# Two inverse matrices, the Fourier branch behind the first two at twice the pace, norm loads on ACT's queue, and an earlier recurrence

## The chip, the cores and the metric

One NeuronCore of a Trainium2 chip runs the whole layer. The metric is device time in microseconds (us) of one launch, lower is better. TensorE is the matmul engine (PE, its weight loads PEld), VectorE is DVE, ScalarE is ACT, GpSimd is POOL; SyncE (SP) starts most DMAs. Each engine works through its own instructions in order.

## What is computed

One layer of a hybrid encoder, 2048 positions, width 1024, all in float32. The normalised input goes through one projection, whose columns feed three branches:

```python
za, za_gate, z_rwkv, zb_gate, zq, zkv, zkr, zc_gate, z_merge = split_cols(h @ w_in, IN_SPLITS)
ya = fourier_mix(za, fourier_w) * silu(za_gate)         # 2-D DFT, real part, group map
zs = centred_shift(z_rwkv, mu_prev, mu_next)
yb = rwkv7_bidir(zs, ...) * silu(zb_gate)               # delta rule in both directions, then group norm
yc = mla(zq, zkv, zkr, ...) * silu(zc_gate)             # attention, 6 heads
g = sigmoid(z_merge)                                    # one gate per branch
merged = g0 * (ya @ proj_a) + g1 * (yb @ proj_b) + g2 * (yc @ proj_c)
out = rms_norm(x + merged @ w_out) * final_g
```

The scan of `rwkv7_bidir` is, per head and direction, `S = S * w + (S a) b^T + v k^T; y = S r`.

## The kernel before

Matmuls keep float32 precision by splitting operands in a high and a low part and adding three products (`mm3`), or run in float32 directly. A scheduler orders most instructions of each engine by priority over a simulated timeline; `after(n)` lowers (or raises) the priority of what it holds. Inside `manual_schedule` TensorE's order is the order of the program text, so a matmul that isn't ready holds all that follow.

**First part, input projection.** `inproj` loads 128 columns of the weights, splits them on ACT and GpSimd, and `project` makes one tile of 128 columns x 512 positions with 24 matmuls. The last 32 column groups (128 projections) run in `columns`, and other work is interleaved with them by hand: `pace` is called twice in each projection, and with `rate` 1 every second call, with `rate` 2 every call, makes one `step`, which advances the generator at the head of a list to its next `yield`. The generators are, in order, `units`, `recurrence`, and later `rwkv_out` and `phase3_early`.

**units** prepares the scan in chunks of 64 positions. 24 windows (three pairs of heads, eight windows of 256 positions) are worked in both directions: low-rank matmuls from a tile `ul`, decay and keys on ACT, VectorE and GpSimd (`unit_decay`; `kds` sums the keys of both directions for the bonus), gram matrices (`unit_gram`), all written to `X_d` in DRAM. Then come the triangular **inverses**, one for each pair of heads: a matrix M of 128 lanes x 64 x 64 is loaded from `X_d`, 62 pairs of VectorE instructions (`tmp`, `M`) solve it in place, and it is written back from GpSimd's queue. One tile M serves all three. They have low priority (`late`), and three of their steps are made for every step of **fourier**, which runs at rate 1 in the same stretch: two halves of 128 columns, each with folds on VectorE, matmuls with DFT matrices loaded as `dm`, and a gate multiplication.

**Second part, attention.** `phase2` works 96 units of 128 queries: scores for 2048 keys (`sc`, evicted and maximised by VectorE as `S`), exp on ACT, 16 transposes `tp` evicted as `PT` (two of four groups by VectorE, `ptd`, two by ACT), value matmuls `av` in pieces. Two steps are made in each unit. `units` waits twelve of them (`wait2`), then **recurrence** goes through 32 chunks in three steps each (`seq_r`, `seq_u`, `seq_s`, `seq_y`), with X and W loaded a chunk ahead, and sets `merged`. Then **rwkv_out** adds the two directions `y_d`, normalises each head's 64 channels with matmuls for the sums (`mu`, `var`), adds the bonus, multiplies the gate, in eight blocks of 256 positions, six steps each, loads started from SP.

**Third part.** Branch projections, merge gates, output projection, final norm. The change doesn't touch it.

Of the kernel before, what the change touches and what calls it, by code (L numbers as in the profile page):

```python
# [9 lines left out]
F32 = mybir.dt.float32  # L10
# [3 lines left out]
ALU = mybir.AluOpType  # L14
# [76 lines left out]
class Trunk:  # L91
    def __init__(self, tc, ins, out, stop=99):
# [266 lines left out]
    def columns(self):  # L359
# [180 lines left out]
    def units(self):  # L540
        tc, nc = self.tc, self.nc
        with tc.tile_pool(name="un", bufs=1, side="right", reuse_waits="tile") as up, \
# [10 lines left out]
            ul = self.unit_lora(opened[0], 0, up)  # L553
# [4 lines left out]
            for s in range(2 * len(wins) + 2):  # L558
# [5 lines left out]
                if s < 2 * len(wins):  # L564
# [5 lines left out]
                    wps = self.unit_lowrank(w, d, ul, gps)  # L570
                    item = self.unit_decay(w, d, wps, up, ge)
# [3 lines left out]
                if s < 2 * len(wins):  # L575
# [4 lines left out]
                    if s + 1 < 2 * len(wins):  # L580
                        ul = self.unit_lora(opened[n + d], 1 - d, up)
# [4 lines left out]
        with tc.tile_pool(name="inv", bufs=1, side="right", reuse_waits="tile") as ip:  # L586
            self.invs = [self.inverses(ip)]
            self.rate = 1
            for _ in self.fourier():
                for _ in range(3):  # L590
                    self.inv_step()
                yield
            while self.invs:
                self.inv_step()
        while not self.rest:
            yield
        for _ in range(self.wait2):
            yield

    def inv_step(self):  # L600
        if self.invs:
            try:
                next(self.invs[0])
            except StopIteration:
                self.invs.pop(0)
# [32 lines left out]
    def unit_lora(self, w, d, up):  # L638
        lo = up.tile([P, 2, UN], F32R, tag="ul", name=f'ul{w["p"]}{w["u"]}{d}', bufs=self.ulb)
        self.nc.sync.dma_start(lo.bitcast(F32), self.lo_d[:, d, :, w["sl"]].rearrange("n p t -> p n t"))  # L640
        return lo
# [9 lines left out]
    def unit_decay(self, w, d, wps, up, ge):  # L651
# [84 lines left out]
    def inverses(self, ip):  # L736
        nc, tc = self.nc, self.tc
        M = ip.tile([P, C, C], F32, name="M")
        tmp = ip.tile([P, 1024], F32, name="tmp")
        diag = M.rearrange("p s t -> p (s t)")[:, ::C + 1]  # L740

        def lanes(p, k):
            d, h, c = k // 4, k // 2 % 2, k % 2 * 16
            return (M[16 * k:16 * k + 16],
                    self.X_d[d][c:c + 16, :, p, 4 * C:5 * C].rearrange("c (h s) t -> c h s t", h=2)[:, h])

        for k in range(8):
            m, x = lanes(0, k)
            nc.sync.dma_start(m, x)
            yield  # L750
        for p in range(NP):
            with self.after(self.late):
                nc.gpsimd.memset(diag, 1.0)
            for j in range(1, C - 1):
                n = C - 1 - j
                with self.after(self.late):
                    tv = tmp[:, 0:j * n].rearrange("p (c i) -> p c i", i=n)
                    nc.vector.tensor_tensor(tv, M[:, 0:j, j:j + 1].to_broadcast([P, j, n]),  # L758
                                            M[:, j:j + 1, j + 1:C].to_broadcast([P, j, n]), ALU.mult)
                    nc.vector.tensor_tensor(M[:, 0:j, j + 1:C], M[:, 0:j, j + 1:C], tv, ALU.add)  # L760
                if j % 3 == 0:
                    yield
            with self.after(self.late):
# [733 lines left out]
```

## Time and profile before

| what | value |
|---|---|
| time, median of 3 runs (lowest to highest) | 2627.77 us (2625.58 to 2630.97) |
| time of the profiled execution | 2634.32 us, of which the span of the instructions is 2632.5 us |
| TensorE busy | 2504.7 us, 95% of the span |
| VectorE, ACT, GpSimd busy | 1737.4, 991.9, 848.0 us |
| TensorE clock granted, mean | 0.982 of full speed |
| DMA | 404.86 MB, mean 154 GB/s |

Busy time of TensorE is that of pipelined matmuls, so a busy engine need not be at its peak. Columns is the stretch from about 480 to 1402 us, attention from 1402 to 2263, the third part from there to the end.

### The profile page before, as it was taken

What the parts mean: (1) busy time and instruction counts of PE and PEld (TensorE: products, weight loads), DVE (VectorE), ACT (ScalarE), POOL (GpSimd) and SP (SyncE); (2) the same over time, 40 slices, a digit from 0 to 9 for tenths busy, and PEclk for the clock granted to TensorE, in tenths of its full rate; (3) what the DMA queues carried; (4) which work ended last, traced back from release to release, by engine and by line L of the source; (5) the groups of instructions that cost most, each with busy time, mean ns of one, the idle gap of its engine ahead of it and who ended that gap; (6) DMA issues with size and microseconds to landing.
All of it is one profiled execution on the core that took longest, in us unless ns stands there. A gap on an engine that the chain in (4) does not pass through costs nothing.

```text
span 2632.5 us, 46308 instructions
## 1 busy us (share of the span) xinstructions
PE 2504.7 (95%) x17295; PEld 2040.8 (78%) x17295; DVE 1737.4 (66%) x3432; ACT 991.9 (38%) x1929; POOL 848.0 (32%) x1124
## 2 busy tenths in 40 slices
PE   7989999999999999989998899999998899999998
PEld 6778887877777777768776688878876677799997
DVE  6236564388888859579398567766767787544444
ACT  6354443355555521111113333333355565322221
POOL 2244433355555511212220233323322220334342
PEclk9999999999999999999998899999999999999999
DMA  4353434477777774552733655665544311645452
GB/s 167 95 146 121 149 125 157 141 262 256 245 262 247 246 156 128 130 145 86 136 84 111 157 169 186 192 186 166 174 149 125 101 53 59 194 128 154 131 154 78
DMA packets 318443, 404.86 MB, mean 154 GB/s; under 512 B 56078, under 2 KB 225097, under 8 KB 317130
## 3 DMA queue, kind: packets, MB, share of 16 engines
q1 hardware_dynamic: 310762, 382.99, 49.0%
q0 software_dynamic: 7456, 18.91, 3.0%
q8 instruction: 137, 2.24, 0.4%
q14 instruction: 88, 0.72, 0.1%
HBM read 236.91 MB, written 164.89 MB: 153 GB/s over the span
## 4 chain that ended last, share of the span: by engine, by line
PE 38%; DVE 13%; DMA 8%; issue 4%; POOL 1%; ACT 1%; SPq 1%; DVEq 0%; POOLq 0%; ACTq 0%
PE av L1334 5%; PE tp L1322 4%; DVE M L760 4%; DVE tmp L758 4%; PE sc L142 3%; PE sc L144 2%; PE sc L143 2%; PE po L144 2%; PE po L143 2%; PE po L142 2%; PE p L144 2%; PE p L143 2%; PE p L142 2%; DVE S L1307 1%; PE mm L142 1%
## 5 line engine op out<-in xcount | busy, mean ns | idle before, releaser
L142 PE MATMUL mm<-hh,wh 128*128 128x512 f32 x1536 | 613.8, 400 | 6.5 <-ACT z L483 3.2
L144 PE MATMUL mm<-hh,wl 128*128 128x512 f32 x1536 | 604.0, 394 | 2.8 <-POOL wl L419 2.6
L143 PE MATMUL mm<-hl,wh 128*128 128x512 f32 x1536 | 605.2, 394 | 0.0
L142 PEld LDWEIGHTS mm<-hh,wh 128*128 128x128 f32 x1536 | 291.7, 190 | 72.1 <-ACT z L483 5.2
L144 PEld LDWEIGHTS mm<-hh,wl 128*128 128x128 f32 x1536 | 291.6, 190 | 65.1 <-POOL wl L419 4.1
L143 PEld LDWEIGHTS mm<-hl,wh 128*128 128x128 f32 x1536 | 291.9, 190 | 58.2 <-issue 1.0
L1307 DVE TENSOR_SCALAR_CACHE_REDUCE S<-sc 128x512 f32<-128x512 f32 x384 | 260.7, 688 | 73.2 <-PE sc L144 67.5
L419 POOL TENSOR_TENSOR wl<-wr,wh 128x256 fp32r<-128x256 f32 x192 | 172.2, 910 | 419.1 <-ACT wh L418 406.2
L1322 PEld LDWEIGHTS tp<-c_id,S 128*128 128x128 f32 x1536 | 192.9, 143 | 84.9 <-ACT PT L1033 14.5
L1322 PE MATMUL tp<-c_id,S 128*128 128x128 f32 x1536 | 237.8, 278 | 21.0 <-ACT S L1314 8.6
L1314 ACT ACTIVATE S<-S,m 128x2048 f32<-128x2048 f32 x96 | 192.2, 2003 | 161.7 <-DVE m L1312 161.7
L758 DVE TENSOR_TENSOR tmp<-M 128x62 f32<-128x62 f32 (+30 forms) x186 | 171.7, 923 | 96.5 <-DMA zm_d<-z 41.3
L142 PE MATMUL sc<-K,Q 96*128 96x512 f32 x384 | 188.4, 491 | 19.7 <-DVE S L1307 13.8
L1033 ACT ACTIVATE PT<-tp 128x512 f32<-128x512 f32 x192 | 113.2, 591 | 225.8 <-PE tp L1322 222.7
L1334 PE MATMUL av<-PT,V 128*64 128x256 f32 x1536 | 180.0, 385 | 0.0
L760 DVE TENSOR_TENSOR M<-M,tmp 128x62 f32<-128x62 f32 (+30 forms) x186 | 170.7, 918 | 5.8
L418 ACT ACTIVATE wh<-wr 128x256 fp32r<-128x256 f32 x192 | 74.4, 412 | 238.7 <-DMA wr<-in_w_in_dram 149.2
L144 PE MATMUL sc<-K,Q 96*128 96x512 f32 x384 | 155.4, 405 | 0.0
L143 PE MATMUL sc<-K,Q 96*128 96x512 f32 x384 | 154.8, 403 | 0.0
L483 ACT ACTIVATE z<-mm 128x512 f32<-128x512 f32 (+1 forms) x120 | 70.3, 589 | 217.7 <-PE mm L144 107.2
L1334 PEld LDWEIGHTS av<-PT,V 128*64 128x64 f32 x1536 | 105.4, 137 | 57.8 <-issue 11.2
L1432 POOL TENSOR_TENSOR g<-g 128x256 f32<-128x256 f32 x128 | 98.8, 774 | 143.2 <-DVE g L1430 100.6
(388 smaller groups left out, 4945.4 us busy)
## 6 DMA issues: line engine op xcount, KB each, us to landing
X_d<-X SPq DMA_DIRECT2D x96, 512.0 KB
sX<-X_d SPq DMA_DIRECT2D x64, 768.0 KB
wr<-in_w_in_dram SPq DMA_DIRECT2D x193, 128.0 KB
zm_d<-z SPq DMA_DIRECT2D x96, 256.0 KB
g<-zm_d SPq DMA_DIRECT2D x64, 384.0 KB
uu<-u_d SPq DMA_DIRECT2D x24, 512.0 KB
ul<-lo_d SPq DMA_DIRECT2D x48, 256.0 KB
sW<-V_d SPq DMA_DIRECT2D x128, 96.0 KB
```

What stands on the lines that cost most here:

```text
L142: mm(out, lh, rh, start=start, stop=False)
L143: mm(out, lh, rl, start=False, stop=False)
L144: mm(out, ll, rh, start=False, stop=stop)
L419: nc.gpsimd.tensor_tensor(wl[:, ks, :], wr, wh[:, ks, :].bitcast(F32), ALU.subtract)
L758: nc.vector.tensor_tensor(tv, M[:, 0:j, j:j + 1].to_broadcast([P, j, n]), M[:, j:j + 1, j + 1:C].to_broadcast([P, j, n]), ALU.mult)
L760: nc.vector.tensor_tensor(M[:, 0:j, j + 1:C], M[:, 0:j, j + 1:C], tv, ALU.add)
L1033: return self.nc.scalar.activation(out, src, AF.Copy)
L1307: nc.vector.tensor_scalar(u["S"][:, ks], sc, 1.0, -3.4e38, ALU.mult, ALU.max, accum_out=u["m4"][:, kb:kb + 1])
L1314: nc.scalar.activation(S, S, AF.Exp, scale=SM_SCALE, bias=m4[:, 5:6], accum_out=u["win"]["rs"][:, col:col + 1])
L1322: nc.tensor.transpose(tp[:, k, :], u["S"][:, (4 * g + k) * P:(4 * g + k + 1) * P], self.ident)
L1334: nc.tensor.matmul(av[64 * h:64 * h + 64, 0:QB], self.V[:, k, (2 * hp + h) * 64:(2 * hp + h + 1) * 64], PT[k // 4][:, k % 4, h, :], start= ...
L1432: nc.gpsimd.tensor_tensor(g, g, acc, ALU.add)
```

## The change

The three inverses get two tiles, M0 and M1 (`Ms`). Both are fetched at once when the units are done; the first two inverses run alone, one step at each step of the projections; the third pair's data is fetched into M0 during the second. After a gap of five steps the Fourier branch starts, at rate 2, with some steps added, and one step of the third inverse beside each of its own. `recurrence` starts its loads before it waits, and waits two steps instead of twelve. Loads of X come behind those of W. `ul` is loaded right behind the matmuls that free its buffer. One addition of the keys goes from GpSimd to VectorE. In the norm the loads go to ACT's queue, the addition of the two directions goes to GpSimd, a block ahead, and a step is added in each block. Once the recurrence is done, one of four PT groups is VectorE's instead of two. The scaling of the row sums `rs` moves behind the third piece of the value matmuls. The last gates are written from ACT's queue and projected in another order.

```diff
-        self.wait2 = 12
+        self.wait2 = 2
+        self.gap = 5
...
-        gates = [(O_ZCG + n * P, self.to_gate(self.gc_d[n], self.nc.gpsimd)) for n in range(3)]
+        gates = [(O_ZCG + n * P, self.to_gate(self.gc_d[n], self.nc.scalar)) for n in range(3)]
...
-        for tb in range(NTB):
+        for tbs in ((0, 1), (2, 3)):
             for w, consume in cols:
-                self.project(w, P, tb, consume, True)
+                for tb in tbs:
+                    self.project(w, P, tb, consume, True)
...
                     wps = self.unit_lowrank(w, d, ul, gps)
+                    if s + 1 < 2 * len(wins):
+                        ul = self.unit_lora(wins[n + d], 1 - d, up)
                     item = self.unit_decay(w, d, wps, up, ge)
...
-                    if s + 1 < 2 * len(wins):
-                        ul = self.unit_lora(opened[n + d], 1 - d, up)
...
-            self.invs = [self.inverses(ip)]
             self.rate = 1
+            Ms = [ip.tile([P, C, C], F32, name="M0")]
+            tmp = ip.tile([P, 1024], F32, name="tmp")
+            self.inv_fetch(Ms, 0, nc.sync)
+            yield
+            with tc.tile_pool(name="inv1", bufs=1, side="right", reuse_waits="tile") as ip1:
+                Ms.append(ip1.tile([P, C, C], F32, name="M1"))
+                self.inv_fetch(Ms, 1, nc.sync)
+                yield
+                yield from self.inverse(Ms, tmp, 0)
+                for n, _ in enumerate(self.inverse(Ms, tmp, 1)):
+                    if n == 8:
+                        self.inv_fetch(Ms, 2, nc.sync)
+                    yield
+            for _ in range(self.gap):
+                yield
+            inv = self.inverse(Ms, tmp, 2)
             for _ in self.fourier():
-                for _ in range(3):
-                    self.inv_step()
-                yield
-            while self.invs:
-                self.inv_step()
-        while not self.rest:
-            yield
-        for _ in range(self.wait2):
-            yield
+                next(inv, None)
+                yield
+            for _ in inv:
+                pass
...
-            nc.gpsimd.tensor_tensor(kds, kd, kds, ALU.add)
+            nc.vector.tensor_tensor(kds, kd, kds, ALU.add)
...
+    def inv_fetch(self, Ms, p, queue):
+        for m, x in self.inv_lanes(Ms, p):
+            queue.dma_start(m, x)
+
+    def inverse(self, Ms, tmp, p):
+        nc, M = self.nc, Ms[p % 2]
+        with self.after(self.late):
+            nc.gpsimd.memset(M.rearrange("p s t -> p (s t)")[:, ::C + 1], 1.0)
+        for j in range(1, C - 1):
+            n = C - 1 - j
             with self.after(self.late):
+                tv = tmp[:, 0:j * n].rearrange("p (c i) -> p c i", i=n)
+                nc.vector.tensor_tensor(tv, M[:, 0:j, j:j + 1].to_broadcast([P, j, n]),
+                                        M[:, j:j + 1, j + 1:C].to_broadcast([P, j, n]), ALU.mult)
+                nc.vector.tensor_tensor(M[:, 0:j, j + 1:C], M[:, 0:j, j + 1:C], tv, ALU.add)
+            if j % 3 == 0:
+                yield
+        with self.after(self.late):
+            for m, x in self.inv_lanes(Ms, p):
+                nc.gpsimd.dma_start(x, m)
+        yield
...
+            while not self.rest:
+                yield
+            for _ in range(self.wait2):
+                yield
             for n in range(NCH):
                 self.seq_r(ps, pad, n, cur)
...
-                    nc.sync.dma_start(t, src[:, :, sl].rearrange("n p t -> p n t"))
+                    nc.scalar.dma_start(t, src[:, :, sl].rearrange("n p t -> p n t"))
...
-                nc.vector.tensor_tensor(y, y, y1, ALU.add)
+                if b == 0:
+                    nc.gpsimd.tensor_tensor(y, y, y1, ALU.add)
                 hi, lo = [rp.tile([P, NP, W], F32R, tag=t, name=f"{t}m{b}", bufs=1) for t in ("rhi", "rlo")]
                 self.split(hi, lo, y, nc.gpsimd)
+                yield
...
                 self.blocksums(var, hi, lo)
+                if b + 1 < T // W:
+                    nc.gpsimd.tensor_tensor(nxt[0], nxt[0], nxt[1], ALU.add)
...
-        self.copy(g in self.ptd, dst, tp)
+        self.copy(g in (self.ptd[1:] if self.merged else self.ptd), dst, tp)
...
         def piece(j):
+            if j == 3:
+                nc.vector.tensor_scalar(rs, rs, 2.0, None, ALU.mult)
+                nc.vector.reciprocal(rs, rs)
...
-        nc.vector.tensor_scalar(rs, rs, 2.0, None, ALU.mult)
-        nc.vector.reciprocal(rs, rs)
```

In `fourier` the change sets `self.rate = 2`, takes the first za and eo tiles at the start and loads za before the small weights product, with two steps more behind that product, one more behind the first DFT load and one more behind each DFT product. In `seq_load` the loads of W now stand ahead of those of X.

## Rows read from the trace of the kernel before

**Rows 1.** Windows by stage: time, busy us (instructions) by engine, granted clock, DMA share, GB/s.

```profile
494.00:921.00 427.00, 408.27 (x2461) 335.01 (x2460) 343.72 (x591) 220.36 (x516) 238.96 (x322) 0.99 0.74 246
921.00:1402.00 481.00, 462.88 (x1984) 363.72 (x1982) 351.43 (x395) 76.49 (x161) 91.67 (x97) 0.98 0.55 131
1402.00:1478.00 76.00, 56.23 (x319) 42.99 (x320) 54.72 (x147) 27.11 (x33) 10.21 (x17) 0.84 0.42 93
1478.00:1936.00 458.00, 454.92 (x6000) 368.63 (x5998) 317.84 (x813) 168.83 (x253) 138.92 (x200) 1.00 0.57 171
1936.00:2175.00 239.00, 213.34 (x1415) 160.68 (x1415) 184.88 (x442) 140.04 (x192) 52.85 (x38) 0.96 0.38 106
```

**Rows 2.** The same view, projections with nothing of other work between them.

```profile
1194.70:1276.30 81.60, 81.60 (x362) 67.57 (x361) 59.25 (x63) 13.19 (x28) 22.79 (x22) 1.00 0.39 91
```

**Rows 3.** Waits of TensorE, 494 to 921: us in total, times, longest us.

```profile
PE bp L731 <- DVE kds L682: 12.3, 9, 2.0
PE wps L648 <- DMA ul<-lo_d: 6.2, 8, 1.6
```

**Rows 4.** Tile kds, 494 to 921: min/median/max ns, first and last start us.

```profile
L678 DVE TENSOR_TENSOR kds<-kds,uu x24: 389/393/401, 514.4 to 903.6; 128x256 f32<-128x256 f32 x24
...
L681 POOL TENSOR_TENSOR kds<-kd,kds x24: 796/898/985, 521.0 to 916.4; 128x256 f32<-128x256 f32 x24
```

**Rows 5.** Waits of TensorE, 921 to 1402.

```profile
PE fy L165 <- DMA dm<-in_c_dft_dram: 7.3, 1, 7.3
PE mm L142 <- ACT z L483: 2.9, 2, 2.1
PE mm L144 <- POOL wl L419: 2.6, 1, 2.6
PE mm L142 <- DVE zg L473: 2.3, 1, 2.3
```

**Rows 6.** Lines of VectorE, 921 to 1402: busy us, mean ns, idle before, releasers.

```profile
L758 DVE TENSOR_TENSOR tmp<-M 128x62 f32<-128x62 f32 (+30 forms) x170 | 161.8, 952 | 96.3 <-DMA zm_d<-z 41.3 <-DMA M<-X_d 40.6 <-DMA wr<-in_w_in_dram 9.1
L760 DVE TENSOR_TENSOR M<-M,tmp 128x62 f32<-128x62 f32 (+30 forms) x169 | 159.8, 946 | 5.6
```

**Rows 7.** Chain that ended last, about 1135: start us, us, what.

```profile
1135.07 5.41 DMA dm<-in_c_dft_dram
```

**Rows 8.** Waits of TensorE, 1402 to 1478.

```profile
PE sps L984 <- DMA sW<-V_d: 10.2, 2, 7.4
PE sc L142 <- DVE zg L473: 5.8, 1, 5.8
PE tp L1322 <- ACT S L1314: 3.8, 2, 3.2
```

**Rows 9.** Waits of TensorE, 1936 to 2175.

```profile
PE sc L142 <- DVE S L1307: 13.8, 5, 6.5
...
PE tp L1322 <- DVE PT L1032: 4.4, 8, 2.7
```

**Rows 10.** Lines of VectorE, 1936 to 2175.

```profile
L1032 DVE COPY PT<-tp 128x512 f32<-128x512 f32 x58 | 39.8, 686 | 5.8 <-PE av L1334 5.8
...
L1062 DVE TENSOR_TENSOR ry<-ry,ry 128x768 f32<-128x768 f32 x8 | 8.6, 1074 | 21.7 <-issue 11.2 <-DMA ry<-y_d 10.5
```

**Rows 11.** Waits of VectorE, 1936 to 2175.

```profile
DVE rs L1337 <- ACT S L1314: 10.8, 5, 2.2
```

**Rows 12.** Lines of ACT, 1936 to 2175.

```profile
L1033 ACT ACTIVATE PT<-tp 128x512 f32<-128x512 f32 x58 | 33.9, 588 | 43.8 <-PE tp L1322 40.9 <-PE av L1334 2.9
```

**Rows 13.** Lines of GpSimd, 1936 to 2175.

```profile
L1087 POOL TENSOR_TENSOR ry<-ry,rbv 128x768 f32<-128x768 f32 x8 | 14.7, 1841 | 34.3 <-ACT ry L1085 34.3
```

**Rows 14.** Waits of the SP queue, 1936 to 2175.

```profile
SPq L1050 <- DVE rva L155: 57.1, 5, 19.3
...
SPq L1050 <- POOL ry L1087: 25.0, 5, 6.4
```

**Rows 15.** Waits of TensorE, 2175 to 2263.

```profile
PE tp L1322 <- ACT PT L1033: 5.0, 5, 2.8
```

More of the change, by code (lines that the diff above doesn't have):

```diff
@@ L638, in unit_lora @@
     def unit_lora(self, w, d, up):
-        lo = up.tile([P, 2, UN], F32R, tag="ul", name=f'ul{w["p"]}{w["u"]}{d}', bufs=self.ulb)
-        self.nc.sync.dma_start(lo.bitcast(F32), self.lo_d[:, d, :, w["sl"]].rearrange("n p t -> p n t"))
+        p, u = w
+        lo = up.tile([P, 2, UN], F32R, tag="ul", name=f"ul{p}{u}{d}", bufs=self.ulb)
+        self.nc.sync.dma_start(lo.bitcast(F32), self.lo_d[:, d, :, u * UN:(u + 1) * UN].rearrange("n p t -> p n t"))
         return lo
@@ L734, in unit_bonus @@
         nc.sync.dma_start(self.bv_d[p][:, w["sl"]], bv)
[L736 to L742, printed above, removed]
-            d, h, c = k // 4, k // 2 % 2, k % 2 * 16
[L744 to L749, printed above, removed]
-            yield
-        for p in range(NP):
-            with self.after(self.late):
[L753 to L763, printed above, removed]
-                for k in range(8):
-                    m, x = lanes(p, k)
-                    nc.gpsimd.dma_start(x, m)
-                    yield
-                if p + 1 < NP:
-                    for k in range(8):
-                        m, x = lanes(p + 1, k)
-                        nc.sync.dma_start(m, x)
-                        yield
@@ new lines, in inv_lanes @@
+    def inv_lanes(self, Ms, p):
+        for k in range(8):
+            d, h, c = k // 4, k // 2 % 2, k % 2 * 16
+            yield (Ms[p % 2][16 * k:16 * k + 16],
+                   self.X_d[d][c:c + 16, :, p, 4 * C:5 * C].rearrange("c (h s) t -> c h s t", h=2)[:, h])
+    def inv_fetch(self, Ms, p, queue):
[7 more added lines that the diff above has]
+            n = C - 1 - j
+            with self.after(self.late):
+                tv = tmp[:, 0:j * n].rearrange("p (c i) -> p c i", i=n)
[8 more added lines that the diff above has]
+        yield
@@ L972, in seq_load @@
                                   self.V_d[c * C:(c + 1) * C, :, h, :])
+        for d in range(2):
+            c = n if d == 0 else NCH - 1 - n
+            nc.sync.dma_start(X[:, d].rearrange("p n s t -> p n (s t)"), self.X_d[d][c])
         return X, W
@@ L1098, in fourier @@
                 tc.tile_pool(name="fops", bufs=self.fb, space=PSUM, side="right", reuse_waits="tile") as fps:
+            big = fp.tile([P, T], F32, tag="za", name="za0"), fp.tile([P, 2, H], F32, tag="eo", name="eo0")
             misc = fp.tile([P, Q], F32, name="misc")
@@ L1107, in fourier @@
             nc.sync.dma_start(altc, self.i["c_alt"][:, 0:P].rearrange("a p -> p a"))
+            self.rate = 2
             for n in range(2):
+                za, eo = big if n == 0 else (fp.tile([P, T], F32, tag="za", name="za1"), fp.tile([P, 2, H], F32, tag="eo", name="eo1"))
+                nc.sync.dma_start(za, self.za_d[n])
                 cw = fp.tile([P, 2, P], F32, tag="cw", name=f"cw{n}")
@@ L1117, in fourier @@
                     nc.scalar.activation(cw[gs, :, gs], cp_[gs, 0:P].rearrange("p (a e) -> p a e", a=2), AF.Copy)
-                za = fp.tile([P, T], F32, tag="za", name=f"za{n}")
-                nc.sync.dma_start(za, self.za_d[n])
                 yield
-                eo = fp.tile([P, 2, H], F32, tag="eo", name=f"eo{n}")
+                yield
+                yield
                 ze, zo = eo[:, 0], eo[:, 1]
@@ L1159, in fourier @@
                 yield
+                yield
                 for par in range(2):
@@ L1171, in fourier @@
                             dms = dft(order[order.index(j) + 1])
+                        yield
                         yield
```

9 lines of the change are left out of this document (1 added, 8 removed).

## Prediction

> **What bounds the kernel now.** I read the windows by stage first [rows 1]. TensorE is busy for 408 of 427 us in the second half of the input projection (the stretch with the unit work, 494 to 921 us), 463 of 481 in the rest of it, 56 of 76 where attention starts, 455 of 458 under the recurrence, 213 of 239 under the norm. So TensorE is the bound nearly everywhere, and this change takes no matmul away: it can only fill the holes. How dense TensorE can be is seen where nothing is interleaved: 362 matmuls in 81.6 us, 0.225 us each, so that one projection (24 matmuls) takes 5.4 us and half of one 2.7 [rows 2].
>
> Second view: what TensorE waited for, stage by stage [rows 3, 5, 8, 9, 15]. Third: the granted clock in [rows 1]. It is 2.4 GHz at 1.00; it falls to 1.2 for some microseconds after the longer holes, and a stage's mean tells how much: (1 - clock) times the stretch is 4 us at 494 to 921, 10 at 921 to 1402, 12 at 1402 to 1478 (there partly while TensorE waits anyway, so I count 6) and 10 at 1936 to 2175. What could be had at most is holes plus clock: 18.5 + 4 = 23 us, 15.1 + 10 = 25, 19.8 + 6 = 26 and 18.2 + 10 = 28, with the rows shown. Together 102 us of 2632.5.
>
> **The change part by part.**
>
> *Unit stage.* TensorE waits 12.3 us, 9 times, for kds at the bonus matmul and 6.2 us, 8 times, for the ul load [rows 3]. kds goes VectorE product, GpSimd addition (0.898 us), VectorE product; the change puts the addition on VectorE, where a product of that shape takes 0.393 us [rows 4]. That removes a 0.9 us step and two changes of engine, and lets the last product follow at once instead of behind what VectorE started meanwhile. It costs 24 x 0.39 = 9.4 us of VectorE, which has 427 - 344 = 83 us free in that stage [rows 1]. The longest wait was 2.0 us; 0.5 us and two hand-overs is about that, so I take 10 of 12.3 away (bounds 0 and 12.3). The ul load is issued right behind the low-rank matmuls that free its one buffer, half a projection (2.7 us) earlier; the longest wait for it is 1.6 us. It stays on SP's queue among weight loads, so I take 4 of 6.2 (bounds 0 and 6.2). The clock falls behind these waits: 3 of 4 back. **17 us**, bounds 0 and 23.
>
> *Inverses and Fourier.* VectorE needs 170 x 0.952 + 169 x 0.946 = 322 us for what it does of the inverses in 921 to 1402; 33 of 372 instructions are left for attention's start [rows 6]. It is idle 96.3 us before them, 41 on a z write and 41 on the load of M: one matrix means write out, load, go on. With two, the next matrix is there. By the code: units end at pace 109 of 256; two fetches, 42 steps of inverse and 5 of gap at one projection each take 49 projections; Fourier then has 50 steps at half a projection, so that all but its last step fits into the 128 projections. Two inverses are 2 x 62 x 2 x 0.95 = 236 us against 49 x 5.4 = 265 us; the third, 118 us, has the 25 projections of Fourier (136 us and Fourier's own matmuls) and is ready before attention starts.
>
> What TensorE gains: the 7.3 us for the dft load, which came behind a write and a load of M [rows 5, 7], and the 2.3 on zg and 2.6 on wl at the end. zg waited for VectorE behind inverse instructions; wl is late because the last weights are used one projection after their buffer came free, and the new order of the last eight projections gives one projection, 5.4 us, more. That is 12.2 of holes and about 6 of the clock. What it may lose: the load of a dft tile takes 5.41 us [rows 7] and has two half steps, 5.4 us, as before; between the other steps 2.7 us stand where 5.4 stood, with ACT and VectorE passes between; and both matrices are fetched at once. The nearest row for such a hole is 2.9 us on z; I put two of these and 1 us of clock against it, 7 us. **11 us**, bounds -20 and 25. ACT's queue for the gates' writes I cost at nothing: 12 issues, on an engine busy 76 of 481 us [rows 1].
>
> *Start of attention.* The recurrence's first matmuls wait 10.2 us for their load, because the last inverse ends only then; the first scores wait 5.8 for zg, and two transposes 3.8 for ACT [rows 8]. With the inverses gone from this stretch I take 10.2 to 3 (seq_load now comes three steps ahead of its first use where it came one, and X comes behind W), 5.8 to 2, 3.8 to 3, and 4 of the clock: 16. Against that Fourier's last step lands here: its gate loads share SP's queue with K and V, and VectorE stands in order behind them: 3 us. **13 us**, bounds 0 and 26. The recurrence starts at step 5 of attention instead of 14 and ends 9 steps earlier; it costs the same, since TensorE is full there [rows 1]. The norm has 7 steps for a block instead of 6 and ends at step 160 where it ended at 161: nothing is late behind it.
>
> *Norm under attention.* VectorE stood 21.7 us before the addition y + y1 [rows 10] and 10.8 before the scaling of the row sums [rows 11]; behind it stood the evictions of scores, and TensorE waited 13.8 and 4.4 us for these [rows 9]. The addition goes to GpSimd, a block ahead, at about the 1.84 us of GpSimd's addition of that shape [rows 13] (8 x 1.84 = 15 us on an engine busy 53 of 239); the scaling goes behind three groups of value matmuls. VectorE also loses one of two copies of a unit, 0.686 us each, which ACT takes at 0.588 [rows 10, 12]: over 29 units 20 us off VectorE (185 of 239 busy) and 17 onto ACT (140 of 239). So I take 13.8 to 3, 4.4 to 2, and 7 of 10 of the clock: 20. ACT then copies three of four, and TensorE already waits 5.0 us for ACT's copies at 2175 to 2263 [rows 15]; 4 us more. **16 us**, bounds -15 and 28.
>
> The loads of the norm move to ACT's queue. On SP they waited 57.1 us for VectorE's rva and 25.0 for GpSimd [rows 14], a queue that had time; an engine that evicts has none. Where the schedule puts each behind its producer, ACT waits little; I cost this at nothing and keep it as a rival. The Trainium skill (DMA: Bandwidth & Descriptors, Issuing engines are not separate DMA queues) says that loads started from several engines run on the same 16 DMA engines, and that only issue time is saved. By that rule the loads land no sooner than now; the sum would stay, if GpSimd's block of lead covers them, and fall as in the third rival, if not. No run so far shows a load on ACT's queue.
>
> Sum: 17 + 11 + 13 + 16 = 57 us off the profiled execution's 2634.3: 2577.3, or 2.2%. The median of the runs shown is 2627.8; the same share gives **2571 us**.
>
> **The rivals.**
> 1. *ACT's queue stands still (slower).* 20 loads (five blocks of four) reuse a buffer and wait for a producer two blocks back. If each holds ACT, exp and copies wait and TensorE with them. SP's 82 us of such waits [rows 14] are the ceiling; from 57/20 = 2.9 us each the whole gain is gone. For it: VectorE runs late here. Against: the order is laid out so that a load comes when its producer is done, and 7 steps a block give more room. At 4 us each, 23 us over: 2651. Chance 0.10.
> 2. *Fourier's half steps are too short.* TensorE's order is fixed, so a step that is late is a hole. 50 steps, each 0.5 us late, are 25 us: 2596. For it: two PSUM buffers, and inverse instructions of about 0.95 us between Fourier's on VectorE. Against: steps were added where loads are waited for. 0.13.
> 3. *The loads land no sooner*: the wait moves from VectorE to GpSimd, then ACT's split, then the mean's matmuls. TensorE's 13.8 and the clock's 7 stay, less 3 for the scaling: 18 us back, 2589. For it: the producers' waits stay [rows 14]. 0.07. The page's rule above would make it this case.
> 4. *ACT becomes the bound under the norm*: 140 + 17 us and the issues of 32 loads, in a stretch that is to shrink to some 220; the copies then wait behind exp. The 16 us are gone: 2587. 0.09.
> 5. *The third inverse is not ready*, so the change does not do what it is named for: the 13 us are gone and the recurrence waits as before: 2584. From the figures above it has some 20 us to spare. 0.06.
>
> **How the numbers follow.** The forecast holds 0.55, its own range 2545 to 2598: the terms up or down by about half. Rivals 2 to 5 lie in or just above it, rival 1 above the time before. 8 times in 10: from 2538 (nearly all that [rows 3, 5, 8, 9] allow) to 2626. No change to be told from measurement is within 0.2%, 5 us. Slower than 2633: rival 1 and a tail of 2, 0.12; between, 0.05; faster 0.83.
>
> **What would show it.** Unit stage: no wait for kds, granted clock at 1.00. Inverses: no idle time on M between the first two; third written out before 1402. End of the projection: no wait on wl. First recurrence matmul some four units earlier. Norm: no row of VectorE waiting for y or row sums; ACT's share up, with a row of ACT waiting at the norm's loads only if rival 1 is right. I would be wrong if the Fourier stretch shows a hole at each step, or if exp starts late behind a load.

## The result, and the profile after

| | kernel before | kernel after |
|---|---|---|
| median (lowest to highest) | 2628.1 us (2625.6 to 2631.0) | 2644.7 us (2642.3 to 2650.3) |
| profiled execution, its span | 2634.3, 2632.5 us | 2645.3, 2643.4 us |

The ratio is 1.0066, with a 95% interval of 1.0047 to 1.0085: slower, where 2571 us and a range of 2538 to 2626 had been forecast.

First the windows by stage, with the stages' new borders; they answer to [rows 1].

```profile
core 0: us, PE busy (x) PEld busy (x) DVE busy (x) ACT busy (x) POOL busy (x), PEclk, DMA share, GB/s
490.00:934.00 444.00, 416.24 (x2497) 339.85 (x2496) 355.73 (x621) 220.92 (x521) 225.81 (x299) 0.99 0.72 238
934.00:1437.00 503.00, 457.29 (x1945) 360.44 (x1943) 374.09 (x423) 76.15 (x160) 98.18 (x95) 0.96 0.56 122
1437.00:1500.00 63.00, 55.93 (x552) 45.36 (x554) 40.71 (x111) 22.66 (x31) 11.44 (x19) 0.95 0.57 181
1500.00:1925.00 425.00, 421.18 (x5578) 341.38 (x5574) 295.98 (x756) 158.65 (x236) 129.92 (x187) 1.00 0.57 174
1925.00:2180.00 255.00, 235.88 (x1619) 178.69 (x1614) 177.18 (x459) 167.13 (x240) 67.93 (x46) 0.99 0.36 103
```

The unit stage ends 9 us later, at about 930 us where it was 921. The columns end at 1436.9 us where they ended at 1401.8: 35 us later, 26 of them lost in the rest of the columns. Attention then takes 836 us where it took 861.6, 26 less, and the third part 1.5 us more. The sum, 9 + 26 - 26 + 1.5, is the 10.9 us between the spans but for rounding. So attention gave nearly what was forecast for it (26 of 29), and the columns lost 35 where a gain of 28 had been forecast.

Next, what TensorE waited for in the unit stage (us in total, times, longest), beside [rows 3].

```profile
PE wps L654 <- DMA ul<-lo_d: 10.8, 9, 2.6
PE wps L654 <- DVE bv L739: 6.7, 13, 1.2
PE bp L737 <- DVE kds L688: 5.4, 8, 0.9
```

kds fell from 12.3 to 5.4, but the wait for ul rose from 6.2 to 10.8, and a wait for bv is new. The same view for the rest of the columns, beside [rows 5]:

```profile
PE fy L166 <- DMA dm<-in_c_dft_dram: 17.5, 1, 17.5
PE cwp L166 <- DMA misc<-in_fourier_w_dram: 10.0, 1, 10.0
PE mm L143 <- ACT z L485: 8.4, 1, 8.4
PE mm L143 <- ACT wh L420: 7.4, 1, 7.4
```

Four waits make 43.3 us where the rows of before made 15.1. They lie at three places: z and wh at 966 to 987 us, the Fourier weights (misc) at 1229 to 1239, dm at 1386 to 1403.5. The small wait for zg is gone, that for wl is 0.2 us. VectorE's lines of the inverses, beside [rows 6] (after the bar: idle time before them and what ended it):

```profile
L762 DVE TENSOR_TENSOR M<-M,tmp 128x62 f32<-128x62 f32 (+30 forms) x186 | 173.4, 932 | 6.4
L760 DVE TENSOR_TENSOR tmp<-M 128x62 f32<-128x62 f32 (+30 forms) x186 | 173.4, 932 | 36.6 <-DMA M<-X_d 30.4
```

All 186 pairs now lie ahead of attention, and VectorE's idle time before them fell from 101.9 us (96.3 + 5.6) to 43.0 (36.6 + 6.4): the change does what it is named for. What attention has of it shows at its start, beside [rows 8]:

```profile
PE sps L986 <- DMA sX<-X_d: 4.8, 2, 3.1
PE sc L143 <- DVE zg L475: 1.4, 1, 1.4
```

Last, TensorE and then ACT under the norm (1925 to 2180 us), beside [rows 9] and [rows 14].

```profile
PE tp L1333 <- ACT PT L1035: 11.3, 16, 1.7
PE var L178 <- POOL rlov L804: 6.2, 1, 6.2
```

```profile
ACT S L1325 <- DMA ys_d<-ry: 4.5, 1, 4.5
ACT PT L1035 <- DMA ys_d<-ry: 3.7, 2, 2.6
```

VectorE is no longer what TensorE waits for, but one wait of 6.2 us for GpSimd's split (rlov) is new, and so are the two rows of ACT. L1052's loads reuse the buffer that ry is stored from, and from ACT's queue that wait is ACT's own.

### The profile page after: what moved, and what is told of

Its sections match the earlier page's. It is cut to its first block, busy times and chain, and to the rows that moved or that the text cites. A ratio compares the mean times of both kernels' runs of the same rounds, so it can differ in the third digit from the quotient of the medians.

```text
span 2643.4 us, 46246 instructions
## 1 busy us (share of the span) xinstructions
PE 2495.2 (94%) x17295; PEld 2033.6 (77%) x17295; DVE 1722.1 (65%) x3403; ACT 1012.7 (38%) x1974; POOL 850.8 (32%) x1096
## 5 line engine op out<-in xcount | busy, mean ns | idle before, releaser
L421 POOL TENSOR_TENSOR wl<-wr,wh 128x256 fp32r<-128x256 f32 x192 | 179.6, 947 | 432.7 <-ACT wh L420 403.6
L1035 ACT ACTIVATE PT<-tp 128x512 f32<-128x512 f32 x237 | 137.6, 590 | 196.2 <-PE tp L1333 186.2
L760 DVE TENSOR_TENSOR tmp<-M 128x62 f32<-128x62 f32 (+30 forms) x186 | 173.4, 932 | 36.6 <-DMA M<-X_d 30.4
L143 PE MATMUL sc<-K,Q 96*128 96x512 f32 x384 | 186.0, 484 | 1.4 <-DVE zg L475 1.4
L145 PE MATMUL sc<-K,Q 96*128 96x512 f32 x384 | 153.5, 400 | 0.0
L144 PE MATMUL sc<-K,Q 96*128 96x512 f32 x384 | 152.6, 397 | 0.0
```

The costliest lines, as they stand in the source:

```text
L143: mm(out, lh, rh, start=start, stop=False)
L144: mm(out, lh, rl, start=False, stop=False)
L145: mm(out, ll, rh, start=False, stop=stop)
L421: nc.gpsimd.tensor_tensor(wl[:, ks, :], wr, wh[:, ks, :].bitcast(F32), ALU.subtract)
L1035: return self.nc.scalar.activation(out, src, AF.Copy)
```

## The experiments

Each ratio is to the kernel before, run beside it on the same chip. The changed kernel's own is 1.0066.

### The unit stage: both edits undone, then each alone

```diff
 # e4: both; e5: the first alone; e6: the second alone
-            nc.vector.tensor_tensor(kds, kd, kds, ALU.add)
+            nc.gpsimd.tensor_tensor(kds, kd, kds, ALU.add)
...
-                    if s + 1 < 2 * len(wins):
-                        ul = self.unit_lora(wins[n + d], 1 - d, up)
                     item = self.unit_decay(w, d, wps, up, ge)
...
+                    if s + 1 < 2 * len(wins):
+                        ul = self.unit_lora(wins[n + d], 1 - d, up)
```

> The changed kernel with both edits of the unit stage undone: the addition into kds on GpSimd again, the ul load at its old place. Theory (VectorE's 24 additions make it late for bv, and the earlier ul load comes no earlier because its buffer is free only later): TensorE's waits for ul and bv at the units (17.5 us now) fall to 7 or less, those for kds return to about 12, and the stage ends some 8 to 12 us earlier: 2632 to 2637 us, ratio to the kernel before 1.001 to 1.004. Rival (the longer unit stage comes from elsewhere): the stage's end stays within 3 us, 2642 to 2648.

Measured: 1.0018 (1.0009 to 1.0028), in the theory's range.

> The changed kernel with only the addition into kds back on GpSimd; ul is still loaded early. Undoing both unit edits gave 14 us in the unit stage. Theory (the addition on VectorE makes the product bv late, which frees the PSUM buffer of the low-rank matmuls): TensorE's wait for bv (6.7 us, 13 times) falls below 2 us, kds returns to some 12 us, the wait for ul stays near 10; the stage gains 3 to 6 us, ratio to the kernel before 1.004 to 1.0055. Rival (the 14 us belong to the addition alone, since a late bv also delays what ul waits for): nearly all 14 us come back, ratio 1.001 to 1.002.

Measured: 1.0015 (1.0002 to 1.0028): the rival's number. (By the traces e4's stage ends 12.6 us before the changed kernel's, not 14.) TensorE's waits in the unit stage of this run:

```profile
PE bp L737 <- DVE kds L688: 13.2, 9, 2.0
PE wps L654 <- DMA ul<-lo_d: 3.5, 5, 1.2
```

> The changed kernel with only the load of ul back at its old place; the addition stays on VectorE. Theory (an earlier load does not land earlier, because it is the one buffer's readers and SP's queue that decide): the wait for ul falls from 10.8 to 7 us or less, that for bv stays near 6.7; the stage gains 4 to 8 us, ratio 1.0035 to 1.005. Rival (the wait for ul is a follower of the late VectorE): ul stays at 9 us or more and the time within 0.1% of the changed kernel's, ratio 1.0055 to 1.007.

Measured: 1.0074 (1.0054 to 1.0094), just above the rival's range, and far from the theory's. Its waits:

```profile
PE wps L654 <- DMA ul<-lo_d: 12.8, 11, 2.1
PE wps L654 <- DVE bv L739: 7.0, 15, 1.2
PE bp L737 <- DVE kds L688: 6.3, 8, 0.9
```

My theory split the loss between the two edits; it fell. With the addition on GpSimd, bv is no row in e5 and 0.5 us in e4, and TensorE waits 3.5 us for ul with the early load and 6.2 with the old one (e4). With it on VectorE, the wait for bv is 7 us and that for ul 11 to 13, early or not. The bonus matmul shows it in one row per kernel: how long and when it started first and last (changed kernel, then e5).

```profile
L737 PE MATMUL bp<-kds,blkr x48: 377/378/455, 523.3 to 928.7; 128*128 128x256 f32 x48
```

```profile
L737 PE MATMUL bp<-kds,blkr x48: 377/378/455, 522.1 to 915.2; 128*128 128x256 f32 x48
```

405.4 us against 393.1; in the kernel before it was 393.5 (526.1 to 919.6 us), in e4 394.6, in e6 404.5. The traces of all the kernels here give the scatter: 392.5 to 396.9 us in the eleven with the addition on GpSimd, 404.3 to 407.4 in the seven with it on VectorE. So the addition alone costs 10 to 12 us, and what the early load does (1 us longer with the addition on VectorE, 1.5 shorter on GpSimd) is inside the scatter. Of the 12.3 us between the changed kernel and e5, 6.7 are TensorE idle for longer; 5.6 are the same matmuls taking longer (378.1 us busy against 372.5, granted clock 0.99 against 1.00). Why ul, a DMA, comes later when VectorE does more was not tried; in all these runs SP stands some 80 us for VectorE's X, with the ul loads in the same queue.

### The second matrix's loads

The changed kernel issues sixteen loads in a row, each of 64 x 64 matrices in pieces of 256 bytes. SP's timeline (start, length, line, transfer, count):

```profile
941.05 24.01 SPq L750 DMA_DIRECT2D M<-X_d  x11
965.16 2.52 SPq L486 DMA_DIRECT2D zm_d<-z  x1
967.73 10.06 SPq L750 DMA_DIRECT2D M<-X_d  x5
977.88 2.35 SPq L419 DMA_DIRECT2D wr<-in_w_in_dram  x1
```

One write of z and one weight load stand behind them, and TensorE waits for z at 966 to 974.7 and for wh at 979.4 to 986.8.

```diff
 # e2: M1's loads later in the program text
-                self.inv_fetch(Ms, 1, nc.sync)
                 yield
-                yield from self.inverse(Ms, tmp, 0)
+                for n, _ in enumerate(self.inverse(Ms, tmp, 0)):
+                    if n == 8:
+                        self.inv_fetch(Ms, 1, nc.sync)
+                    yield
 # e7: as e2, and ahead of the loads
+                        with self.after(self.late):
+                            nc.vector.tensor_copy(Ms[1][:, 0, 0:1], Ms[0][:, 0, C - 1:C])
```

> The changed kernel with the eight loads of the second matrix at step 8 of the first inverse instead of one step behind the first matrix's loads. Theory (sixteen loads back to back hold SP's queue for 37 us, so that a z write and a weight load come late): the hole of 18.8 us near 966 to 987 us goes, TensorE waits under 3 us there; the first matrix lands earlier and the inverses end earlier, so that the wait of 10.0 us for the Fourier weights near 1240 shrinks too. 2618 to 2630 us, ratio to the kernel before 0.996 to 1.001. Rival (the hole is of TensorE's clock or of VectorE's first inverse steps, not of SP's queue): the hole stays within 3 us of 18.8 and the time at 2640 to 2650.

Measured: 1.0037 (1.0019 to 1.0054), but the experiment says nothing on the theory (whose hole is 15.8 us by the rows, not 18.8): the scheduler put eleven of the loads back to back all the same (942.6 to 965.9 us), and z was waited for twice, 8.4 and 6.0 us. Moving text does not move a transfer that nothing holds.

> The changed kernel with the loads of the second matrix really held back: a copy of one column from M0 into M1 at step 8 of the first inverse stands ahead of them, so they can start only near 1005 us. In the run with the loads moved in the program text alone, eleven of sixteen still went back to back. Theory (the burst of sixteen loads holds up a z write and a weight load): the two holes of 15.8 us near 966 to 987 us shrink below 4 us in sum, the first matrix lands near 957 instead of 966, the inverses end some 9 us earlier, and the wait for the Fourier weights, 10.0 us, stays between 8 and 18 because TensorE also comes earlier by what was won. 2628 to 2638 us, ratio 0.999 to 1.003. Rival (eight loads alone do the same harm, or the z write waits for something else): the two holes stay above 12 us, ratio 1.005 or more.

Measured: 1.0047 (1.0030 to 1.0063). Waits of TensorE from 934 to 1200 us:

```profile
PE mm L143 <- ACT z L485: 14.9, 2, 12.6
PE mm L143 <- ACT wh L420: 2.0, 1, 2.0
```

Half of each was right. At 967 us only 2.3 us of wait are left, so the sixteen in a row were the cause there; but the eight, now together at 1031 us, made a hole of 12.6 of their own. The next run spreads them, on top of e5.

```diff
 # e11: e5, and in the first inverse
+                    if n % 3 == 2 and lanes:
+                        g = slice(n // 3 * 32, n // 3 * 32 + 32)
+                        with self.after(self.late):
+                            nc.vector.tensor_copy(Ms[1][g, 0, 0:1], Ms[0][g, 0, C - 1:C])
+                        for m, x in lanes[:2]:
+                            nc.sync.dma_start(m, x)
+                        lanes = lanes[2:]
```

> The changed kernel with the addition into kds back on GpSimd, and the loads of the second matrix two at a time behind steps 2, 5, 8 and 11 of the first inverse, each pair held back by a copy of one column. When eight loads were held back together, the hole moved with them (12.6 us near 1031) and only one of the two at 966 to 987 went. Theory (it is a run of eight or more loads, each 2.5 us of issue with full DMA engines, that a z write and a weight load stand behind): with pairs the waits for z and weights between 940 and 1080 us sum to 5 us or less instead of 16.8; the wait for the Fourier weights grows to 12 to 22 us, since TensorE comes 17 us earlier and the matrix is written out only some 8 us earlier. Ratio to the kernel before 0.997 to 1.000. Rival (each pair costs its own hole): those waits sum to 12 us or more, ratio 1.001 or more.

Measured: 0.9996 (0.9982 to 1.0009), some 5 us better than e5, though the two intervals overlap. Waits from 934 to 1200 us:

```profile
PE mm L143 <- ACT wh L420: 8.3, 1, 8.3
PE mm L143 <- ACT z L485: 4.2, 2, 2.7
```

Between 940 and 1080 us 4.2 us are left of the 16.8 in e5, as the theory says. The 8.3 for wh are another place, at 1100 us: TensorE now comes 10 us earlier than in e5 to the stretch where M0 is written out and filled again, and a weight load is 6.7 us in issue there. The wait for the Fourier weights stayed at 10.1, where 12 to 22 were expected.

### The dft tiles at the end of the columns

SP's timeline and GpSimd's before the wait of 17.5 us:

```profile
1372.95 2.91 SPq L1287 DMA_DIRECT2D K<-kn_d  x2
1375.91 2.79 SPq L1288 DMA_DIRECT2D K<-kr_d  x1
...
1388.50 0.32 SPq L1271 DMA_DIRECT2D Q<-qr_d  x1
1393.62 3.09 SPq L1163 DMA_DIRECT2D dm<-in_c_dft_dram  x2
```

```profile
1364.50 6.05 POOL L767 DMA_DIRECT2D X_d<-M  x8 [4.01 <-DVE M L762]
```

Fourier's last steps need dm while K and Q are loaded for the first scores and the third matrix is written out. Two theories, one of the queue's order and one of the DMA engines.

```diff
 # e3
-                        nc.sync.dma_start(dm, self.i["c_dft"]...
+                        nc.scalar.dma_start(dm, self.i["c_dft"]...
 # e8: after the last pair of dft loads, and ahead of K's first loads
+                    if n == 1 and j == 3:
+                        nc.gpsimd.tensor_copy(self.eps[:, 4:5], dms[0][:, 0, 0:1])
...
+                if hp == 0:
+                    nc.gpsimd.tensor_copy(kt[:, 0, 0, 0:1], self.eps[0:96, 4:5])
```

> The changed kernel with the loads of the dft tiles started from ACT's queue instead of SP's. Theory (the last dft loads stand behind K and Q loads on SP's queue, which wait for buffers and for DMA): the wait of 17.5 us for dm near 1390 falls below 6 us, 2622 to 2632 us, ratio to the kernel before 0.998 to 1.002. Rival (the 16 DMA engines are taken by the third inverse's write-out and by K and Q, and the queue that starts a load does not matter): the wait stays at 12 us or more, 2640 to 2648 us, ratio 1.005 to 1.008.

Measured: 1.0053 (1.0038 to 1.0068); the wait for dm is 16.5 us. The theory of SP's order fell. But the rival isn't shown by this either, since the load also started late. TensorE had last read dm's buffers at 1383 us, and ACT had nothing ahead of the load, yet ACT started it only at 1397.04, just behind the landing of a load of K (1396.96). In the changed kernel SP started it at 1393.62, just behind the landing of the same load (1393.56). SP's waits there, 1370 to 1410 us:

```profile
SPq L1163 <- DMA K<-kn_d: 4.7, 1, 4.7
SPq L1163 <- DMA K<-kr_d: 2.2, 1, 2.2
```

In these traces the DMAs that SP and ACT start report their landing on eight semaphores in turn, shared by both, and a start waits until the last DMA on its semaphore has landed; for the two dm loads these were two loads of K. Of the 17.5 us, 7.6 pass before the first load starts and 9.9 while it is under way; the last of the third matrix's eight writes lands at 1395.9 (1399.0 in this run). The Trainium skill (DMA: Bandwidth & Descriptors, Issuing engines are not separate DMA queues) says that all loads run on the same 16 DMA engines whichever engine starts them; this run agrees (17.5 us became 16.5), but with the late start it can't show it.

> The changed kernel with the first loads of K held back until the last pair of dft tiles has begun to land, by two copies of one column on GpSimd. Moving the dft loads to ACT's queue left the wait at 16.5 us. Theory now (3 MB of K and 2 MB of the third matrix's write-out fill the 16 DMA engines from 1364 to 1397 us, and the dft load stands behind them whichever queue starts it): without K in between the wait for dm falls from 17.5 us below 6, and the first scores wait 3 to 10 us for K instead; 2630 to 2640 us, ratio 1.000 to 1.004. Rival (the third matrix's write-out alone, 640 packets of small pieces on each engine, is what the load waits for): the wait stays above 12 us and the scores wait on top, ratio 1.006 to 1.010.

Measured: 1.0041 (1.0025 to 1.0057), not clear of the changed kernel's own interval. Waits from 1200 to 1437 us:

```profile
PE cwp L166 <- DMA misc<-in_fourier_w_dram: 9.3, 1, 9.3
PE fy L166 <- DMA dm<-in_c_dft_dram: 6.9, 1, 6.9
```

dm fell from 17.5 to 6.9 us, just short of the theory's 6, and the first scores started 7.6 us late instead (a row that names no releaser; by the edit it is K). The load of dm starts at 1388.6 us now, waits for no K, and is under way for 9.1 us. K was part of it, by that start; the rest was left to e16, below. The write-out has 640 packets in all, not on each engine: in the changed kernel, from 1360 to 1410 us, its 2.10 MB take 29% of the engines' time, where the 5.31 MB that SP started take 40%.

### Norm and gates

```diff
 # e1: the kernel before with attention's edits: ACT-queue norm loads, the GpSimd
 #     addition, one step more, ptd[1:] when merged, rs behind piece 3
 # e9: e1 with
-                    nc.scalar.dma_start(t, src[:, :, sl].rearrange("n p t -> p n t"))
+                    nc.sync.dma_start(t, src[:, :, sl].rearrange("n p t -> p n t"))
 # e13: the same line in the changed kernel
 # e10: e1 with the change's two edits of the last gates (ACT's queue, halves)
```

> The kernel before with the edits of attention alone: norm loads on ACT's queue, the addition y + y1 on GpSimd a block ahead, one step more for a block, one transpose copy more on ACT, the scaling of the row sums behind three groups of value matmuls. Units, inverses, Fourier, gate writes, the order of W and X and the start of the recurrence stay as in the kernel before. Theory (the third and fourth terms of the sum were sound in kind, and the loss lies in the columns stage): TensorE's holes for S and PT under the norm shrink, 10 to 20 us off the profiled execution, 2610 to 2620 us, ratio 0.993 to 0.997. Rival (the norm edits themselves cost: ACT's queue stands still or ACT becomes the bound): ratio 1.000 or more, with ACT waiting at the norm's loads.

Measured: 0.9960 (0.9944 to 0.9976). Attention's edits pay, but with a cost that ACT's rows show (1935 to 2175 us; TensorE's first):

```profile
PE tp L1326 <- ACT PT L1033: 12.0, 13, 2.5
```

```profile
ACT PT L1033 <- DMA ys_d<-ry: 5.1, 2, 3.0
ACT S L1318 <- DMA ys_d<-ry: 4.1, 1, 4.1
```

> The kernel of the run with attention's edits alone, its norm loads back on SP's queue; the addition on GpSimd a block ahead, the copies and the row sums stay changed. Theory (the gain of that run came from taking the late producers off VectorE; the queue that starts the loads matters little, since SP had time): TensorE's holes for S and PT under the norm stay within 3 us of that run's, ratio to the kernel before 0.9945 to 0.997. Rival (the loads on ACT's queue come sooner and this is what the gain rests on): GpSimd's addition waits for the loads, half or more of the 10.5 us is lost, ratio 0.998 to 1.000.

Measured: 0.9931 (0.9906 to 0.9956), better still. TensorE, then GpSimd:

```profile
PE tp L1326 <- ACT PT L1033: 5.6, 10, 1.7
```

```profile
POOL ry L1083 <- DMA ry<-y_d: 22.0, 4, 8.5
```

Neither theory had this. ACT's two waits are gone. GpSimd waits 22 us for the loads, as the rival said, but it works a block ahead, and TensorE's only row for GpSimd is 0.5 us.

> The changed kernel with the norm's loads back on SP's queue, nothing else. Theory (ACT stands at these loads until the block's result is stored, and its copies of PT stand behind them): ACT's waits for the store of ry go, TensorE's wait for ACT's PT copies falls from 14.0 us to 8 or less, attention takes 5 to 10 us less, ratio to the kernel before 1.003 to 1.005. Rival (with the recurrence five units earlier the norm has room and the queue costs nothing here): ratio 1.0055 to 1.0075.

Measured: 1.0030 (1.0018 to 1.0042); TensorE's wait for ACT's PT fell from 11.3 us (not 14.0) to 7.5 in the same stretch, and no row of ACT names ry's store. So the queue costs the changed kernel 0.36% too, about 9 us. (The intervals of e1 and e9 overlap, and by a little those of e12 and e15, below; this pair's don't.) The Trainium skill (DMA: Bandwidth & Descriptors, Anatomy of one DMA) says that a DMA's semaphore wait is made by the sequencer that issues it; the rows agree, and on ACT that sequencer is also the one of the copies.

> The kernel before with attention's edits and the two edits of the last gates (written from ACT's queue, projected by halves of the positions). Theory: the waits for zg and wl at the end of the columns (2.3 and 2.6 us) go and part of the 5.8 us before the first scores, with some of the clock: 4 to 9 us better than attention's edits alone, ratio 0.9925 to 0.9945. Rival (the writes on ACT's queue hold its copies, or zg just waits elsewhere): ratio 0.9955 to 0.9975.

Measured: 0.9941 (0.9918 to 0.9963): the theory's range, but the interval overlaps e1's. In the traces the columns end 6 us earlier than in e1, of which 4.0 are a shorter wait for dm (5.5 us against 9.5) that these edits don't touch, and TensorE waits 8.6 us for zg before the first scores where it waited 5.9. The row for wl is gone; zg still has 2.3 us in the columns.

### Mended kernels

```diff
 # e12: e11, K held back as in e8 but head by head (first head behind the pair j == 1), and
-        self.gap = 5
+        self.gap = 7
...
                     nc.scalar.activation(cw[gs, :, gs], ...
                 yield
-                yield
-                yield
 # e15: e12, norm loads on SP.  e16: e15 without
-            for m, x in self.inv_lanes(Ms, p):
+            for m, x in self.inv_lanes(Ms, p) if p < 2 else ():
                 nc.gpsimd.dma_start(x, m)
 # e14: e9 with the two edits of the gates
```

> The run before it, and: the loads of K for the first head behind the landing of the third last pair's dft tile and those of the second head behind the last pair's (both by copies of one column on GpSimd), two steps fewer behind the weights of each Fourier half, and a gap of seven instead of five. Theory (the holes of the columns come from three stretches of full DMA engines and of matrices that finish late, and each can be taken away): wait for z and weights 5 us or less, for the Fourier weights 5 to 12, for dm below 6, for K below 5; the columns end at 1385 to 1400 us instead of 1437, and with attention's 26 us kept the time is 2600 to 2618, ratio 0.988 to 0.994. Rival (what is taken away in one place comes back at the next transfer, since DMA itself has no room there): the columns still end after 1410 us, ratio 0.997 or more.

Measured: 0.9972 (0.9959 to 0.9985): the rival's range. The waits from 1200 to 1437 us:

```profile
PE fy L166 <- DMA dm<-in_c_dft_dram: 11.7, 1, 11.7
PE pp L166 <- issue: 2.9, 1, 2.9
PE sc L143 <- issue: 2.8, 1, 2.8
```

The Fourier weights are no longer waited for. Of the edits between e11 and e12 only the gap bears on that place, so two projections of room were what lacked there; whether they do without the loads in pairs was not run. But dm is waited for 11.7 us, and the columns end at 1414.

> The mended kernel (second matrix's loads in pairs, K held back, gap of seven, addition into kds on GpSimd) with the norm's loads on SP's queue. Theory: 5 to 10 us better than with them on ACT's queue, ratio 0.9935 to 0.9955. Rival (no cost of the queue where the norm starts early): 0.9965 to 0.998.

Measured: 0.9948 (0.9933 to 0.9963): the theory's range, 6 us better than e12.

> The run before it without the eight writes of the third matrix; the recurrence of the third pair of heads then reads what was there before the inverse, so a part of the result is left out. Theory (2 MB in small pieces fill the DMA engines while the dft tiles wait behind them): the wait for dm falls from 11.7 us below 3, and the time falls by 8 to 14 us against the run before it, ratio 0.988 to 0.992. Rival (K, Q and the dft tiles fill the DMA engines by themselves): the wait stays above 8 us and the time within 4 us of the run before it.

Measured: 0.9868 (0.9851 to 0.9885). No row of dm is left:

```profile
PE sps L994 <- DMA sX<-X_d: 4.4, 2, 2.7
PE sc L143 <- issue: 3.6, 1, 3.6
PE pp L166 <- issue: 2.4, 1, 2.4
```

dm's load lands 4.5 us after its start, where it took 15.1 in e15. So the third matrix's write-out was the rest of the wait for dm. The time fell by 0.8%, 21 us, more than the 8 to 14 expected. In the profiled traces the last twelve projections take 17 us less, of which 11.8 are this wait; the rest I can't place beyond the intervals of both runs.

> The kernel before with the edits that paid alone: attention's edits with the norm's loads left on SP's queue, and the two edits of the last gates. Theory (the two gains lie in different stages and add up): 0.9931 for the first and 6 to 9 us for the second give a ratio of 0.989 to 0.992, 2604 to 2612 us. Rival (the gates' gain of the run with ACT's queue was taken there by chance or is eaten by the norm's earlier start): 0.993 or more.

Measured: 0.9902 (0.9887 to 0.9918), median 2603.5 us: the theory's range. The gates' part, 0.3%, is no larger than the intervals, here and in e10, so that the two gains add up is likely and not shown. This version, without any edit of units or inverses, beats both kernels; only e16, which leaves work out, took less. What the second matrix or the earlier recurrence would give alone was not run.

## Why the prediction was wrong

**Unit stage: -17 us forecast (bounds on the gain 0 and 23), +9 measured. The step that failed** is that 24 x 0.39 us of VectorE lie beside other work because it "has 427 - 344 = 83 us free in that stage". The addition took 0.425 us, and kds did come earlier (12.3 to 5.4, where I took 10 away). But free time on the average of a stage is none within a unit: bv, next on VectorE, frees the buffer that the low-rank matmuls write, and those waited 6.7 us for it. e5 and e6 put 10 to 12 us on this edit. The other term, 4 us for the early ul load, is not borne out: the wait is 2.7 us less between e4 and e5, but the stage's length stays within its scatter.

**Inverses and Fourier: -11 forecast, bounds -20 to 25 on the gain; +26 measured, beyond the bound. The step that failed** is the fit of two inverses, 236 us, into 49 projections, 265 us. It counted VectorE alone. The first inverse begins only when its matrix has landed (941 to 966.5 us, 25 us), and Fourier's buffers reuse M1's memory, so that its first loads wait for the write-out of M1 (issued from 1211 us, landed from 1217.5 to 1235.8, about 25 us). 236 + 50 is 286, not 265. Holes I had priced at "two of these" at 2.9 us; they were 15.8, 10.0 and 17.5, each with a fall of the granted clock (0.64 at 979 to 989 us, 0.55 at 1240 to 1245, 0.58 at 1400 to 1410, where 1.00 is 2.4 GHz and 0.50 the lower level of 1.2). I did write that "both matrices are fetched at once", but priced no wait behind them on SP's queue: e7 and e11 show that it is these loads. And I took Fourier's end to be free but for its last step; e8 and e16 show that its last dm tiles wait for 3 MB of K, whose landing holds their start, and for the third matrix's write-out, which fills the DMA engines.

**Start of attention: -13 forecast.** The recurrence's waits fell from 10.2 to 4.8 us, zg from 5.8 to 1.4, the transposes from 3.8 to 0.9. By unit 60 of attention, with the recurrence over in both kernels, the lead is 12.7 us: as forecast.

**Norm: -16 forecast.** VectorE's holes went as described: TensorE's 13.8 and 4.4 us for it are no rows any more, and the lead grows by another 13 us to attention's end. **The step that failed here** is the move of the loads, which I "cost at nothing": it costs 9 us (e13), and the same edits without it took 0.69%, 18 us, off the kernel before (e9). The view of [rows 14] had a row that I didn't count in the ceiling of 82 us:

```profile
SPq L1050 <- DMA ys_d<-ry: 12.2, 5, 3.5
```

This wait for ry's store is the one that later stood on ACT (8.2 us in the changed kernel, 9.2 in e1).

**The rivals.** The first, ACT's queue standing still, had the right place and mechanism, at 9 us, where 57 would have been needed to take the whole gain; that its 2651 us lie near the 2645 measured is chance. The second, half steps too short all along, was not seen: the Fourier stretch shows two long holes and 2.1 us in three short ones, nothing at each step. The third came in one row at most: GpSimd's block of lead covers its wait for the loads in e9, but in the changed kernel TensorE waits 6.2 us for GpSimd's split (3.3 in e13), and what delayed it was not tried. Of the fourth a part is seen, since TensorE's largest wait under the norm is now ACT's copies, 7.5 us even with the loads on SP (e13); it did not take the gain. The fifth was not so: the third inverse's last VectorE instruction is done by 1364 us. The cases that happened, transfers of the matrices in the way and a late bv, were among none of them.

## What to carry to other kernels

When work moves to an engine, look for that engine's next result inside one round of the loop, not for its idle time over the stage. When a buffer's reuse is part of a chain, its load and its write-out are terms of the sum like the computing, and whatever stands behind them on the same queue or the same DMA engines can be late too. A load's start can also wait for the landing of a load that it has nothing to do with: the queue's own waits tell this, TensorE's don't. A load that may have to wait belongs on the queue of an engine that does nothing else.

## What the runs showed of the hardware

Transfers in pieces of 256 bytes fill the DMA engines at a low rate: from 941 to 978 us of the changed kernel, with 14366 of 14550 packets under 512 bytes, the engines are 9 tenths busy or more from the third slice of forty to the last, and move 108 GB/s; from 1380 to 1400 us, with K, Q, dm and the last of the third matrix's writes under way, full engines (shares of 1.01 and 1.03) move 254 to 272 GB/s. And a start takes longer while the engines are full: SP needs 0.33 us for the first load at 941 us and 2.2 us on the mean of the first eleven (24.01 / 11), and a weight load takes 2.35 us to start at 977.9 us and 0.38 at 988.2, so that a queue of sixteen loads is a stretch of 37 us in which nothing else of SP starts on time.
